# Retention: weighting the normed rows before the value projection, with the context's keys of all heads made first

## The chip, the cores and the metric

The kernel runs on one core of a Trainium2 chip. The metric is the device time of one execution in microseconds: the median of three runs of the kernel before is 1511.96 us (1507.57 to 1512.51). One further execution was taken with the hardware profiler; all durations below are from that one.

## The reference

Two transformer blocks of two layers each work on 256 tokens of 1024 features, in fp32. The first block (attention of four sorts, cross attention to a memory, a gated MLP with a short convolution) and most of the second (gated feed-forward layers, a convolution mixer) are not touched. The change lies in the first mixer of the second block, the retention. Cut to what matters:

```
ax = modulate(rms_norm(hx), ...)           # 256 x 1024, the tokens
ac = modulate(rms_norm(ctx), ...)          # 256 x 1024, the context
q, k, v, g = split(ax @ w_qkvg)            # 4 heads: q, k 256 wide, v, g 512 wide
kc, vc     = split(ac @ w_qkvg[:, D:4*D])  # keys and values of the context
q, k = rope(q), rope(k)
o = (q k^T * decay) v + (q kc^T * decay_ctx) vc       # per head, both directions
y = (silu(g) * o * rsqrt(mean(o*o) + eps)) @ w_o
hx = hx + g1 * y
```

Since v = ax @ Wv and vc = ac @ Wv with one matrix Wv, o is also ((q k^T * decay) ax + (q kc^T * decay_ctx) ac) @ Wv.

## The kernel before

Everything is kept feature-major: 1024 features are 8 tiles of 128 partitions, with the 256 tokens on the free axis. Each fp32 factor of a product is held as two tiles, a rounded high part (suffix h) and the rest (suffix l), and mm3 issues three TensorE products per tile: high with high, high with low, low with high.

Weights stream from HBM in pieces of 128x1024 in the order that `_plan` (L47) writes out by hand. SP loads a piece into one of five raw buffers (`Stream.dma`, L357). `Stream.split` (L369) makes the two parts: ScalarE copies to `wh`, VectorE subtracts to `wl`, into four slots; `Stream.get` (L386) hands a piece to the products and splits up to two or three pieces further ahead. A piece of 256 output columns holds four of the eight feature tiles, so a projection takes two pieces: `fm` (L487) does its 48 products into one PSUM bank, `fm_apart` (L492) into two banks, with some products 258 columns wide. `kouter` (L534) adds 48 products of an output matrix to the four accumulators. PSUM has four more banks for everything else (tag mm).

`after_piece` (L426) runs after each piece: it takes the next function from the list `hooks`, and every second piece it issues one product of the modulation parameters on VectorE (`ada_one`, L410, tile adaj) with its load.

The retention (from L1321) makes the normed rows `axs` of the tokens first, on ScalarE and VectorE with raised priority (`pre`, L1281, called at L1359). The context's rows `cxs` are there from the layer before. Then, for each of four heads: the load of the decay table `dec` (512 KB); keys and the first half of the values of both row sets with `both` (L1388), one piece serving `cxs` and `axs` in turn; the keys' rope; q and its rope; the second half of the values; the gates with Silu into `sg`; and as hooks, spread over the pieces that follow, the five steps of `ret_attention` (L1432): scores times decay (`ath`, `atl`), the weighted values in two halves, their norm's sums over single-column products, and the finish (the norm's factor spread by two small transposes, `sg` scaled and split into `soh`, `sol`). `ret_out(h - 1)` is called at the end of head h. In the first head `both` takes its four pieces at once (ahead) and does all of `cxs` ahead of all of `axs`.

The order within an engine is set by a planner when the program is built: it takes ready instructions by priority, which is the order in which the code issues them, apart from the raised ones.

Of the kernel before, what the change touches and what calls it, by code (L numbers as in the profile page):

```python
# [18 lines left out]
T = 256  # L19
# [27 lines left out]
def _plan():  # L47
# [29 lines left out]
    perm = _np.concatenate([half, half + 64])  # L77
    for h in range(4):
        add([("ret_w_qkvg_2", 0, 1024 + 256 * h + perm)], _ALL_K)
        for e in range(2):  # L80
            add([("ret_w_qkvg_2", 0, 2048 + 512 * h + 256 * e + _np.arange(256))], _ALL_K)
            if e == 0:
                add([("ret_w_qkvg_2", 0, 256 * h + perm)], _ALL_K)
        for e in range(2):
            add([("ret_w_qkvg_2", 0, 4096 + 512 * h + 256 * e + _np.arange(256))], _ALL_K)
        if h:
            for e in range(2):
                add([("ret_w_o_2", 0, _np.arange(D))], [4 * (h - 1) + 2 * e, 4 * (h - 1) + 2 * e + 1])
    for e in range(2):
        add([("ret_w_o_2", 0, _np.arange(D))], [12 + 2 * e, 13 + 2 * e])  # L90
# [184 lines left out]
def tile_two_blocks(ctx, tc, aps, out):  # L275
# [26 lines left out]
    def tt(out, a, b, op):  # L302
        V.tensor_tensor(out=out, in0=a, in1=b, op=op)  # L303
# [17 lines left out]

    X = cst_p.tile([128, KD, T], F32, name="X")
    CST = cst_p.tile([128, _NCST], F32, name="CST")
    VEC = cst_p.tile([128, _NVEC], F32, name="VEC")
    IDB = cst_p.tile([128, 128], BF16, name="IDB")
    MEMR = cst_p.tile([128, 2], F32, name="MEMR")
    CAUS = cst_p.tile([128, 128], BF16, name="CAUS")
# [4 lines left out]
    def cst(n):  # L332
        o, w = _CST[n]
        return CST[:, o:o + w]

# [4 lines left out]
    ones, ident, slt = cst("ones"), cst("ident"), cst("slt")  # L340
    ones_slt = CST[:, _CST["ones"][0]:_CST["ones"][0] + 256]

# [218 lines left out]
    WIDE, NARROW = 7 * (T + 64) + T + 64, 8 * T  # L561
# [107 lines left out]
    nc.sync.dma_start(out=CST, in_=aps["cst"])  # L669
# [125 lines left out]
    def layer(i, xs, nrm, last_gain, background=None, second=None):  # L795
        with ExitStack() as es:
# [210 lines left out]
            def fillers():  # L1007
# [4 lines left out]
                for t in range(2):  # L1012
                    act(VFX[:, t, :], o[t][:, 0:256], AF.Copy, scale=nrm.r[:, t:t + 1])
                    v = cp.tile([128, 128], F32, tag="vct", name="vct", bufs=2)
                    act(v, o[t][:, 256:384], AF.Copy, scale=nrm.r[:, t:t + 1])
                    vcs.append(v)
# [302 lines left out]
    cxs = box["cxs"]  # L1319

# [44 lines left out]
    def fm_part(o, e, h, l, n, xs):  # L1365

        hv = h.rearrange("p (k n c) -> p k n c", k=4, n=2)
        lv = l.rearrange("p (k n c) -> p k n c", k=4, n=2)
        for k4 in range(4):
            k = 4 * e + k4  # L1370
            for t in range(2):
                mm3(o[:, t * T:(t + 1) * T], hv[:, k4, t, :], lv[:, k4, t, :], xs[0](k), xs[1](k),
                    k == 0 and t == 0, k == 7)

    def tok_part(o, e, h, l, n, xs):

        hv = h.rearrange("p (k c) -> p k c", k=4)
        lv = l.rearrange("p (k c) -> p k c", k=4)
        for k4 in range(4):
            k = 4 * e + k4  # L1380
            for t in range(2):
                a, b = (x(k, t * 128, (t + 1) * 128) for x in xs)
                ov = o[:, t * 256:(t + 1) * 256]
                mm(ov, a, hv[:, k4, :], start=k == 0 and t == 0)
                mm(ov, a, lv[:, k4, :])
                mm(ov, b, hv[:, k4, :], stop=k == 7)

    def both(parts, ahead=False):  # L1388

        if ahead:  # L1390
            st.hold = st.n_get
            ws = [[st.get() for e in range(2)] for _ in parts]
            os_ = [[bank(), bank()] for _ in parts]
            for x, xs in enumerate((cxs, axs)):
                for f, w, o in zip(parts, ws, os_):
                    for e in range(2):
                        f(o[x], e, *w[e], xs)
                        if x:
                            after_piece()
            st.hold = None  # L1400
            return os_
        out = []
        for f in parts:
            o = [bank(), bank()]
            for e in range(2):
                w = st.get()
                for x, xs in enumerate((cxs, axs)):
                    f(o[x], e, *w, xs)
                after_piece()
            out.append(o)  # L1410
        return out

    def pair_tiles(tag, shape, bufs=1):
        at = 64 if tag in ("q", "at") else 128
        return [rp.tile(shape, F32R, tag=tag + e, name=tag + e, bufs=bufs, at=at) for e in "hl"]

    def rope2(tag, o):
        out = rp.tile([128, 2, T], F32, tag="ropo", name="ropo", bufs=1)
        a = rp.tile([128, 2, T], F32, tag="ropa", name="ropa", bufs=1)
# [12 lines left out]
    def ret_attention(h, q, kx, kc, vx, vc, sg, dec):  # L1432
        box_ = {}

        def scores():
            ath, atl = box_["at"] = pair_tiles("at", [128, 4, T], 1)
            for e, (kh, kl) in enumerate((kx, kc)):
                o = bank()
                for kt in range(2):
                    c = slice(kt * 128, kt * 128 + 128)  # L1440
                    for ab in range(2):
                        mm3(o[:, kt * T:(kt + 1) * T], kh[:, ab, c], kl[:, ab, c], q[0][:, ab, :], q[1][:, ab, :], kt == 0 and ab == 0, ab == 1)
                w = slice(2 * e, 2 * e + 2)
                at = rp.tile([128, 2, T], F32, tag="at", name="at")
                tt(at, o.rearrange("p (k t) -> p k t", k=2), dec[:, w, :], ALU.mult)
                split_psum(ath[:, w, :], atl[:, w, :], at)

        def values(e):
            ath, atl = box_["at"]
            o = bank()  # L1450
            for d2 in range(2):
                d = 2 * e + d2
                for kt in range(4):
                    vh, vl = (t[:, kt % 2, d * 128:(d + 1) * 128] for t in (vx, vc)[kt // 2])
                    mm3(o[:, d2 * T:(d2 + 1) * T], vh, vl, ath[:, kt, :], atl[:, kt, :], d2 == 0 and kt == 0, kt == 3)
            sq = rot_p.tile([128, 2, T], F32, tag="sq", name="sq")
            act(sq, o.rearrange("p (n t) -> p n t", n=2), AF.Square)
            box_["sq", e] = sq
            tt(sg[:, 2 * e:2 * e + 2, :], o.rearrange("p (n t) -> p n t", n=2), sg[:, 2 * e:2 * e + 2, :], ALU.mult)

        def sums():
            ss = rot_p.tile([128, 2, T], F32, tag="ss", name="ss")
            tt(ss, box_["sq", 0], box_["sq", 1], ALU.add)
            p = bank()
            for t in range(2):
                for e in range(2):
                    mm(p[:, t:t + 1], ss[:, e, t * 128:(t + 1) * 128], ones[:, 0:1], start=t == 0 and e == 0, stop=e == 1)
            box_["r"] = rsqrt(p[:, 0:2], 1.0 / 512.0)

        def finish():  # L1470
            R = spread(box_["r"])
            soh[h] = rp.tile([128, 4, T], F32R, tag="soh", name="soh", at=64)
            sol[h] = rp.tile([128, 4, T], F32R, tag="sol", name="sol", at=64)
            for e in range(2):
                q = slice(2 * e, 2 * e + 2)
                tt(sg[:, q], sg[:, q], R.unsqueeze(1).to_broadcast([128, 2, T]), ALU.mult)
                act(soh[h][:, q], sg[:, q], AF.Copy)
                tt(sol[h][:, q], sg[:, q], soh[h][:, q].bitcast(F32), ALU.subtract)

        return [scores, lambda: values(0), lambda: values(1), sums, finish]  # L1480

# [5 lines left out]

    for h in range(4):
        dec = rp.tile([128, 4, T], F32, tag="dec", name="dec", bufs=1)
        nc.sync.dma_start(out=dec, in_=aps["dec"][h].rearrange("p (k t) -> p k t", k=4))  # L1490
        kc, vx, vc = pair_tiles("kc", [128, 2, T]), pair_tiles("vx", [128, 2, 512]), pair_tiles("vc", [128, 2, 512])

        def keep_values(e, oc, ox):
            for v, o in ((vc, oc), (vx, ox)):
                split_psum(*(t[:, :, 256 * e:256 * e + 256] for t in v), o.rearrange("p (k c) -> p k c", k=2))


# [280 lines left out]
```

## Time and profile before

| | |
|---|---|
| median of three runs | 1511.96 us |
| the profiled execution | 1513.38 us, span 1511.6 us |
| TensorE products | busy 1478.4 us of the span, 12130 products |
| VectorE | busy 1185.9 us, 2297 instructions |
| ScalarE | busy 810.6 us, 1441 instructions |
| DMA | 292.95 MB, mean 194 GB/s |
| mean granted TensorE clock | 0.992 |

Times are microseconds from the start of the span. PE is TensorE, DVE is VectorE, ACT is ScalarE, SP is the engine that issues the loads. A product's duration is longer than the distance to the next one, because products overlap, so TensorE's busy time does not tell its rate; the distance of starts does.

### The profile page before, as it was taken

To read this page: it belongs to the slowest core of one execution; us is meant where nothing else is said; L and a number is where in the kernel's file an instruction comes from. 1 tells how busy PE (TensorE), PEld (TensorE's weight loads), DVE (VectorE), ACT (ScalarE), POOL (GpSimd) and SP (SyncE) were. 2 spreads that over 40 slices of the span, in tenths; PEclk is the share of its full clock that TensorE was granted. 3 is DMA by queue.
4 is the path that set the end of the run, shared out by engine and by line. 5 is a ranking of instruction groups with operands and counts; after the bars stand their busy time and mean duration, and the time that the engine had idled before them with its cause. 6 is when DMAs were issued, how large, how long until landed. Compare 5 with 4: busy or idle time off the path is not lost.

```text
span 1511.6 us, 30254 instructions
## 1 busy us (share of the span) xinstructions
PE 1478.4 (98%) x12130; PEld 1416.1 (94%) x12130; DVE 1185.9 (78%) x2297; ACT 810.6 (54%) x1441; POOL 0.2 (0%) x4
## 2 busy tenths in 40 slices
PE   8999999999999999999999999999999999999997
PEld 6877899999886889999999999999999999999997
DVE  7677789998888789999785766668977788885555
ACT  7455676565656467576543434335544465564443
POOL 0000000000000000000000000000000000000000
PEclk9999999999999999999999999999999999999998
DMA  8621446776562266587544656456788866556651
GB/s 299 223 78 31 150 169 207 251 239 205 190 223 85 89 204 227 180 273 266 184 165 168 194 169 209 153 183 208 261 297 290 296 186 191 182 181 196 195 190 64
DMA packets 81212, 292.95 MB, mean 194 GB/s; under 512 B 9136, under 2 KB 9136, under 8 KB 80944
## 3 DMA queue, kind: packets, MB, share of 16 engines
q1 hardware_dynamic: 81072, 291.03, 58.7%
q8 instruction: 95, 1.56, 0.4%
q14 instruction: 45, 0.37, 0.1%
HBM read 289.94 MB, written 1.05 MB: 193 GB/s over the span
## 4 chain that ended last, share of the span: by engine, by line
PE 88%; DVE 5%; DMA 3%; ACT 3%; issue 1%; SPq 0%; DVEq 0%; ACTq 0%
PE mm L297 58%; PE a L297 28%; DMA raw<-in_w_dram 2%; PE a L760 1%; DVE wl L303 1%; ACT wh L320 1%; DVE ss L303 1%; DVE xl L312 1%; DMA memx<-in_mem_dram 1%; DMA w<-in_cw_dram 1%; ACT xh L320 0%; DVE X L303 0%; DVE y L312 0%; ACT y L320 0%; ACT PT L761 0%
## 5 line engine op out<-in xcount | busy, mean ns | idle before, releaser
L303 DVE TENSOR_TENSOR wl<-raw,wh 128x1024 fp32r<-128x1024 f32 (+2 forms) x440 | 532.6, 1214 | 175.5 <-ACT wh L320 172.4
L320 ACT ACTIVATE wh<-raw 128x1024 fp32r<-128x1024 f32 (+2 forms) x440 | 459.9, 1050 | 346.1 <-PE mm L297 170.9
L297 PE MATMUL mm<-xh,wh 128*128 128x256 f32 (+1 forms) x2064 | 574.6, 279 | 2.7 <-ACT fj L320 2.6
L297 PE MATMUL mm<-xl,wh 128*128 128x256 f32 x2064 | 576.0, 279 | 0.0
L297 PE MATMUL mm<-xh,wl 128*128 128x256 f32 (+1 forms) x2064 | 573.6, 279 | 0.0
L297 PEld LDWEIGHTS mm<-xh,wh 128*128 128x128 f32 x2064 | 389.0, 189 | 3.9 <-ACT fj L320 3.0
L297 PEld LDWEIGHTS mm<-xl,wh 128*128 128x128 f32 x2064 | 389.2, 189 | 1.3 <-DVE xl L312 0.6
L297 PEld LDWEIGHTS mm<-xh,wl 128*128 128x128 f32 x2064 | 388.8, 189 | 0.0
L312 DVE SCALAR_TENSOR_TENSOR adaj<-adaw,CC 128x1024 bf16<-128x1024 f32 x112 | 136.4, 1218 | 0.1
L297 PE MATMUL mm<-wh,xh 128*128 128x256 f32 (+3 forms) x384 | 119.2, 311 | 7.0 <-ACT wh L320 7.0
L297 PE MATMUL mm<-wl,xh 128*128 128x256 f32 (+3 forms) x384 | 118.9, 310 | 0.0
L297 PE MATMUL mm<-wh,xl 128*128 128x256 f32 (+3 forms) x384 | 118.5, 309 | 0.0
L297 PE MATMUL a<-sh,wl 128*128 128x256 f32 x352 | 97.3, 276 | 1.3 <-DVE wl L303 1.3
L297 PE MATMUL a<-sh,wh 128*128 128x256 f32 x352 | 97.2, 276 | 0.0
L297 PE MATMUL a<-sl,wh 128*128 128x256 f32 x352 | 97.2, 276 | 0.0
L297 PE MATMUL a<-fsl,wh 128*128 128x256 f32 x352 | 96.9, 276 | 0.0
L297 PE MATMUL a<-fsh,wh 128*128 128x256 f32 x352 | 96.8, 276 | 0.0
L297 PE MATMUL a<-fsh,wl 128*128 128x256 f32 x352 | 96.6, 276 | 0.0
L297 PEld LDWEIGHTS mm<-wh,xh 128*128 128x128 f32 x384 | 72.8, 190 | 10.8 <-ACT wh L320 7.0
L312 DVE SCALAR_TENSOR_TENSOR y<-U,VEC,y 128x256 f32<-128x256 f32 x176 | 74.7, 479 | 4.6 <-ACT y L320 4.3
L297 PEld LDWEIGHTS mm<-wl,xh 128*128 128x128 f32 x384 | 72.7, 189 | 4.0 <-DVE wl L303 0.8
L297 PEld LDWEIGHTS mm<-wh,xl 128*128 128x128 f32 x384 | 72.7, 189 | 2.5
(308 smaller groups left out, 2422.0 us busy)
## 6 DMA issues: line engine op xcount, KB each, us to landing
raw<-in_w_dram SPq DMA_DIRECT2D x424, 512.0 KB, 4.1
adaw<-in_ada_dram SPq DMA_DIRECT2D x96, 512.0 KB, 4.5
raw<-in_w_dram SPq DMA_DIRECT2D x8, 416.0 KB, 4.0
raw<-in_w_dram SPq DMA_DIRECT2D x8, 384.0 KB, 4.4
memx<-in_mem_dram SPq DMA_DIRECT2D x4, 512.0 KB, 4.6
w<-in_cw_dram SPq DMA_DIRECT2D x4, 512.0 KB, 5.2
dec<-in_dec_dram SPq DMA_DIRECT2D x4, 512.0 KB, 4.5
X<-in_x_dram SPq DMA_DIRECT2D x4, 256.0 KB, 5.1
```

The costliest lines, as they stand in the source:

```text
L297: nc.tensor.matmul(out, lhsT, rhs, start=start, stop=stop, skip_group_check=True)
L303: V.tensor_tensor(out=out, in0=a, in1=b, op=op)
L312: return V.scalar_tensor_tensor(out=out, in0=a, scalar=s, in1=b, op0=op0, op1=op1, accum_out=accum_out)
L320: A.activation(out=out, in_=a, func=func, scale=scale, **kw)
L760: nc.tensor.transpose(pt[:, b:b + 128], Ps[u][:, h, kt * 128:(kt + 1) * 128], ident)
```

## The change

The values are no longer projected. Per head the scores weight the normed rows themselves: `weighted_rows` adds, over four tiles of tokens (two of `axs`, two of `cxs`), row tile times weight, for eight feature tiles, and splits the sums into the two parts `Y`. `values` then projects `Y` with the value weights by `fm`. For this the rows are needed with tokens on the partitions: `token_rows` transposes both parts of both row sets on TensorE, in groups of four 128x128, and ScalarE (high part) and VectorE (low part) copy them to `ctok` and `atok`.

The context's keys of all heads are made first, from their own copies of the key pieces; `kcs` keeps them. The key weights of each head are so streamed twice: the plan of this stage has 72 pieces instead of 64. The order within a head is then own keys, q, output of the head before (heads 1 and 2), scores, first gates, weighting, second gates, values; the outputs of heads 2 and 3 come last. The norm's sums and the finish remain hooks, now in the next head's keys and q. `fm_apart` remains for q of heads 0 and 2.

To make room, `dec` is half as large and loaded in two halves, the second into the same buffer after the first was used; the rope's buffers are those of the weighted scores (tag at); the gates lie in q's tiles; `soh` and `sol` lie in those of `Y`, for head 2 in those of the first context keys; `atok` lies in the rows' pool, in a slot whose tiles are 64 columns longer. The constants are split in two tiles and two loads, of which the second tile lives until the first block ends. In the first block, `vct` takes buffers of tag tok.

```diff
@@ _plan: order of the weights
+    for h in range(4):
+        keys(h)
     for h in range(4):
-        add([("ret_w_qkvg_2", 0, 1024 + 256 * h + perm)], _ALL_K)
-        for e in range(2):
-            add([("ret_w_qkvg_2", 0, 2048 + 512 * h + 256 * e + _np.arange(256))], _ALL_K)
-            if e == 0:
-                add([("ret_w_qkvg_2", 0, 256 * h + perm)], _ALL_K)
...
+        keys(h)
+        add([("ret_w_qkvg_2", 0, 256 * h + perm)], _ALL_K)
+        if h in (1, 2):
+            ret_out(h - 1)
+        gates(h, 0)
+        gates(h, 1)
+        vals(h, 0)
+        vals(h, 1)
+    ret_out(2)
+    ret_out(3)
...
+    def token_rows(xs, tok, t, kk):
+
+        for part, (x, o) in enumerate(zip(xs, tok)):
+            p = bank()
+            for j in range(4):
+                nc.tensor.transpose(p[:, j * 128:(j + 1) * 128], x(4 * kk + j, t * 128, (t + 1) * 128).bitcast(F32), ident)
+            w = o[:, t * D + kk * 512:t * D + kk * 512 + 512]
+            if part:
+                V.tensor_copy(out=w, in_=p)
+            else:
+                A.copy(out=w, in_=p)
...
+    def weighted_rows(ath, atl, Y):
+
+        for p in range(4):
+            o = bank()
+            for f2 in range(2):
+                f = slice((2 * p + f2) * 128, (2 * p + f2 + 1) * 128)
+                for kt in range(4):
+                    h, l = (t[:, (kt % 2) * D:(kt % 2 + 1) * D][:, f] for t in (atok, ctok)[kt // 2])
+                    mm3(o[:, f2 * T:(f2 + 1) * T], h, l, ath[:, kt, :], atl[:, kt, :], f2 == 0 and kt == 0, kt == 3)
+            split_psum(Y[0].pair(2 * p), Y[1].pair(2 * p), o.rearrange("p (n t) -> p n t", n=2))
...
+    for h in range(4):
+        if h % 2 == 0:
+            kc = half_tiles(f"kc{h}", [128, 4, T], 128)
+        o = fm(cxs)
...
+        split_psum(*kcs[h], o.rearrange("p (n t) -> p n t", n=2))
+        token_rows(cxs, ctok, h // 2, h % 2)
+
+    atok = [x.t[:, 16:16 + 2 * D] for x in xs_tiles()]
...
     for h in range(4):
...
+        kx = rope2("kx", fm(axs))
+        if h == 0:
+            for kk in range(2):
+                token_rows(axs, atok, 0, kk)
+        q = rope2("q", fm_apart(axs) if h % 2 == 0 else fm(axs))
         flush()
+        if h == 0:
+            for kk in range(2):
+                token_rows(axs, atok, 1, kk)
+        if h in (1, 2):
             if accs is None:
                 accs = four()
             ret_out(h - 1)
+        ath, atl = half_tiles("at_", [128, 4, T], 64)
+        scores(0, q, kx, decs[0], ath, atl)
+        nc.sync.dma_start(out=decs[1], in_=aps["dec"][h].rearrange("p (k t) -> p k t", k=4)[:, 2:4, :])
+        scores(1, q, kcs[h], decs[1], ath, atl)
+
+        sg = [t.bitcast(F32) for t in half_tiles("q", [128, 2, T], 64)]
+        act(sg[0], fm(axs).rearrange("p (n t) -> p n t", n=2), AF.Silu)
+        Y = tuple(Rows(t) for t in half_tiles("Y", [128, KD * T], 64))
+        weighted_rows(ath, atl, Y)
+        act(sg[1], fm(axs).rearrange("p (n t) -> p n t", n=2), AF.Silu)
+        sqs, box_ = [], {}
+        for e in range(2):
+            values(e, Y, sg, sqs)
+        hooks.append(lambda sqs=sqs, b=box_: sums(sqs, b))
+        hooks.append(lambda: None)
+        hooks.append(lambda h=h, sg=sg, b=box_: finish(h, sg, b))
+    ada_state["rate"] = 0
+    ret_out(2)
     flush()
```

## Rows read from the trace of the kernel before

**Rows 1.** The page: busy time by engine, and the chain that ended last, by engine.
```profile
PE 1478.4 (98%) x12130; PEld 1416.1 (94%) x12130; DVE 1185.9 (78%) x2297; ACT 810.6 (54%) x1441; POOL 0.2 (0%) x4
...
PE 88%; DVE 5%; DMA 3%; ACT 3%; issue 1%; SPq 0%; DVEq 0%; ACTq 0%
```

**Rows 2.** Stretches: length, busy us (instructions) of each engine, clock, DMA share, GB/s.
```profile
700.00:740.00 40.00, 40.00 (x356) 40.00 (x355) 36.06 (x60) 24.00 (x37) 0.00 (x0) 1.00 0.70 229
750.60:1036.80 286.20, 285.47 (x2462) 284.51 (x2462) 196.94 (x348) 110.15 (x153) 0.00 (x0) 1.00 0.55 178
755.00:772.60 17.60, 17.60 (x149) 17.37 (x149) 15.94 (x57) 7.59 (x15) 0.00 (x0) 1.00 0.28 88
```

**Rows 3.** Groups by line, 757 to 1042: count, busy us, mean ns, idle before.
```profile
L297 PE MATMUL mm<-wh,xh 128*128 128x256 f32 x256 | 71.2, 278 | 0.0
...
L297 PE MATMUL mm<-ath,vxh 128*128 128x256 f32 x32 | 8.9, 277 | 0.0
```

**Rows 4.** TensorE's timeline: start, us, engine, line, operation, tiles; ends of four stretches.
```profile
750.64 0.28 PE L297 MATMUL mm<-xh,wh 128*128 128x256 f32 x1
...
868.65 0.28 PE L297 MATMUL a<-soh,wh 128*128 128x256 f32 x1
...
871.37 0.28 PE L297 MATMUL mm<-ath,vxh 128*128 128x256 f32 x1
...
894.68 0.28 PE L297 MATMUL mm<-wh,xh 128*128 128x256 f32 x1
...
905.99 0.28 PE L297 MATMUL mm<-xh,wh 128*128 128x258 f32 x1
...
1036.82 0.28 PE L297 MATMUL mm<-xh,wh 128*128 128x258 f32 x1
```

**Rows 5.** TensorE's timeline: four transposes among wide products, in another stage.
```profile
405.26 0.60 PE L879 MATMUL mm<-CST,q 128*128 128x128 f32 x4
405.61 0.48 PE L297 MATMUL mm<-wh,xh 128*128 128x512 f32 x1
405.93 0.39 PE L297 MATMUL mm<-wl,xh 128*128 128x512 f32 x1
406.16 0.39 PE L297 MATMUL mm<-wh,xl 128*128 128x512 f32 x1
```

**Rows 6.** Line 879: the transposes' durations, ns min/median/max, first and last start.
```profile
L879 PE MATMUL mm<-CST,q x16: 272/273/312, 33.8 to 407.3; 128*128 128x128 f32 x16
```

**Rows 7.** TensorE's timeline: a norm's sums and the product behind them.
```profile
882.25 0.94 PE L297 MATMUL mm<-CST,ss 128*128 128x1 f32 x8
883.06 0.36 PE L297 MATMUL mm<-xh,wh 128*128 128x256 f32 x1
```

**Rows 8.** Groups by line of VectorE, 757 to 1042.
```profile
L312 DVE SCALAR_TENSOR_TENSOR adaj<-adaw,CC 128x1024 bf16<-128x1024 f32 x30 | 36.6, 1219 | 0.1
L303 DVE TENSOR_TENSOR ropo<-mm,RT 128x256 f32<-128x256 f32 x16 | 6.7, 418 | 2.8 <-PE mm L297 2.8
...
L303 DVE TENSOR_TENSOR ropo<-ropo,ropa 128x512 f32<-128x512 f32 x8 | 5.5, 687 | 0.1
```

**Rows 9.** VectorE's timeline at the start of the stage.
```profile
754.46 0.69 DVE L303 TENSOR_TENSOR ss<-ss,sq 128x512 f32<-128x512 f32 x1
...
770.59 2.06 DVE L312 SCALAR_TENSOR_TENSOR X<-X,VEC,R 128x256 f32<-128x256 f32 x5
...
777.58 3.49 DVE L303 TENSOR_TENSOR wl<-raw,wh 128x1024 fp32r<-128x1024 f32 x3
```

**Rows 10.** The tile dec: its loads, from issue to landing.
```profile
DMA to landing us min/median/max: 4.2/4.5/4.7
```

**Rows 11.** SP's timeline in the middle of the stage: issues of weight loads.
```profile
879.29 6.39 SPq L365 DMA_DIRECT2D raw<-in_w_dram  x2
```

**Rows 12.** Stretches behind the retention, columns as in rows 2.
```profile
1054.00:1058.00 4.00, 2.02 (x16) 1.82 (x15) 3.69 (x7) 2.87 (x9) 0.00 (x0) 0.97 1.01 377
1058.00:1062.00 4.00, 4.00 (x24) 4.00 (x23) 3.65 (x9) 0.06 (x1) 0.00 (x0) 0.61 0.96 321
```

More of the change, by code (lines that the diff above doesn't have):

```diff
@@ L1363, in tile_two_blocks @@
         stt(X[:, k, :], X[:, k, :], gf[:, k:k + 1], nrm.R, ALU.mult, ALU.mult)
[L1365 to L1411, printed above, removed]
@@ L1428, in rope2 @@
         return hl
-    soh, sol = {}, {}
[L1432 to L1480, printed above, removed]
@@ new lines, in token_rows, with scores @@
+    def token_rows(xs, tok, t, kk):
[8 more added lines that the diff above has]
+                A.copy(out=w, in_=p)
+    def scores(e, q, keys, dec, ath, atl):
+        kh, kl = keys
+        o = bank()
+        for kt in range(2):
+            c = slice(kt * 128, kt * 128 + 128)
+            for ab in range(2):
+                mm3(o[:, kt * T:(kt + 1) * T], kh[:, ab, c], kl[:, ab, c], q[0][:, ab, :], q[1][:, ab, :], kt == 0 and ab == 0, ab == 1)
+        w = slice(2 * e, 2 * e + 2)
+        at = rp.tile([128, 2, T], F32, tag="at", name="at")
+        tt(at, o.rearrange("p (k t) -> p k t", k=2), dec, ALU.mult)
+        split_psum(ath[:, w, :], atl[:, w, :], at)
@@ L1486, in ret_out, with values @@
             kouter(lambda f: (soh[h][:, 2 * e + f, :], sol[h][:, 2 * e + f, :]), accs, h == 0 and e == 0, h == 3 and e == 1)
-    for h in range(4):
[L1489 to L1495, printed above, removed]
-        a, b = both([fm_part, tok_part], h == 0)
-        split_psum(*kc, a[0].rearrange("p (n t) -> p n t", n=2))
-        kx = rope2("kx", a[1])
-        keep_values(0, *b)
-        q = rope2("q", fm_apart(axs))
-        keep_values(1, *both([tok_part])[0])
-        sg = rp.tile([128, 4, T], F32, tag="sg", name="sg", bufs=1)
+    def values(e, Y, sg, sqs):
+        o = fm(Y)
+        sq = rot_p.tile([128, 2, T], F32, tag="sq", name="sq")
+        act(sq, o.rearrange("p (n t) -> p n t", n=2), AF.Square)
+        sqs.append(sq)
+        tt(sg[e], o.rearrange("p (n t) -> p n t", n=2), sg[e], ALU.mult)
@@ new lines, in sums, with finish @@
+    def sums(sqs, box_):
+        ss = rot_p.tile([128, 2, T], F32, tag="ss", name="ss")
+        tt(ss, sqs[0], sqs[1], ALU.add)
+        p = bank()
+        for t in range(2):
+            for e in range(2):
+                mm(p[:, t:t + 1], ss[:, e, t * 128:(t + 1) * 128], ones[:, 0:1], start=t == 0 and e == 0, stop=e == 1)
+        box_["r"] = rsqrt(p[:, 0:2], 1.0 / 512.0)
+    def finish(h, sg, box_):
+        R = spread(box_["r"])
+        if h == 2:
+            soh[h], sol[h] = half_tiles("kc0", [128, 4, T], 128)
+        else:
+            soh[h], sol[h] = (t[:, 0:4 * T].rearrange("p (k t) -> p k t", k=4) for t in half_tiles("Y", [128, KD * T], 64))
+        for e in range(2):
+            q = slice(2 * e, 2 * e + 2)
+            tt(sg[e], sg[e], R.unsqueeze(1).to_broadcast([128, 2, T]), ALU.mult)
+            act(soh[h][:, q], sg[e], AF.Copy)
+            tt(sol[h][:, q], sg[e], soh[h][:, q].bitcast(F32), ALU.subtract)
@@ L1505, in tile_two_blocks @@
+    for h in range(4):
+        decs = []
         for e in range(2):
+            dec = rp.tile([128, 2, T], F32, tag="dec", name="dec", bufs=1)
+            decs.append(dec)
             if e == 0:
-                for f, o in enumerate(fm_apart(axs)):
-                    act(sg[:, f, :], o, AF.Silu)
-            else:
-                act(sg[:, 2 * e:2 * e + 2, :], fm(axs).rearrange("p (n t) -> p n t", n=2), AF.Silu)
-        flush()
-        steps = ret_attention(h, q, kx, kc, vx, vc, sg, dec)
```

59 lines of the change are left out of this document (31 added, 28 removed).

## The prediction

> **What bounds the kernel now.** I read the page first. TensorE is busy for 98% of the span and the chain that ended last runs through it for 88% [rows 1], so time can only be won by giving TensorE less to do or by filling its gaps. Then the table by stretches: the retention stage, 750.6 to 1036.8 us, has TensorE busy for 285.5 of 286.2 us at the full granted clock, with VectorE at 196.9 us (69%) and ScalarE at 110 us [rows 2]. So this stage has no gaps to fill: it is a count of products. The two rows that carry most of what is edited are in the groups by line [rows 3]: 256 products of each of three kinds form the values of both row sets (768 in all), and 32 of each of six kinds weight them (192). Last I read the timeline for the price of a product. The mean of 278 ns in those groups is a latency, since products overlap; what counts is the distance of starts. 24 products of 256 columns start between 868.65 and 871.37, so 113.3 ns each; 96 start between 894.68 and 905.99, so 117.8 ns each [rows 4]. The stream has these two paces. In this stage it falls into the slower one behind single-column sums or small transposes, and comes back while a run of 258-column products (fm_apart) passes.
>
> The stage in full: 2400 products at 113.3 ns are 271.9 us of the 286.2 between 750.64 and 1036.82 [rows 4]. Of the other 14.3 us some 7 are the norms' single-column sums and their spreads (one set of eight takes from 882.25 to 883.06 [rows 7]; there are six such sets and as many spreads), the rest, about 7, is the slower pace.
>
> **The change part by part.**
>
> *Products.* Per head, before: 96 for keys, 192 for values, 48 for q, 96 for gates, 24 for scores, 48 for weighting, 96 for the output, 600 in all. After: 48 for the context's keys, 48 for own keys, 48, 96 and 24 as before, 96 to weight the rows (8 feature tiles x 4 token tiles x 3), 96 for the values of the sums, 96 for the output, 552. Four heads lose 192 products; at 113.3 ns that is -21.8 us, all on the path, since TensorE has no slack.
>
> *Transposes.* Weighting sums over tokens, so the rows must stand with tokens on the partitions: 64 transposes of 128x128, in 16 groups of four. In the trace four transposes hold the stream from 405.26 to 405.61, and the product behind them keeps the next one 0.32 us away instead of 0.23 [rows 5]: 0.44 us per group, +7.0 us. Bounds: 5.6 (nothing behind them) to 17.5 us (64 x 273 ns [rows 6], nothing overlapped). I take the row, which is the same operation among the same kind of products. The Trainium skill ("TensorE: Matmul & The Clock Gate", Part 4: PE-mode transpose) speaks against this part: it measures about 275 ns for one in a kernel, and says that transposes do not keep the clock up. By that, end to end, they would cost 17.6 us and the gain would all but vanish; the row of four in 0.35 us disagrees, so I give this under 2 in 100, inside the case "eaten".
>
> *Pace.* Before, fm_apart runs twice in every head; after, only for q of heads 0 and 2, and in head 0 transposes follow it. The slower pace costs 4.5 ns per product: at most 9.9 us if all 2208 go so, 0 if none. I take two thirds of the most and the runs of 258 with it, 9 us against 7 now: +2.0 us, between -7 and +3.
>
> *The start of the stage.* This is where I expect a gap. Before, the first four weight pieces serve 48 products each, so TensorE lives on them while VectorE makes the normed rows. After, a piece of context keys serves 24 products, 2.7 us. VectorE worked 15.94 us in 755.0 to 772.6 [rows 2], without a single split of weights between 754 and 775. Of that, 15.3 us stay (one 0.6 us key split is counted below). Until piece 8 is split it must add four splits at 1.14 us (three take 3.49 [rows 9]), 4.6 us, and for heads 0 and 1 a key split and a copy of transposed rows each, 4 x 0.6 = 2.4 us. From 755.1 [rows 9] that ends at 777.4 without a pause. TensorE wants piece 8 after 168 products (19.0 us), six groups of transposes (2.6 us) and the norm's sums (1.9 us, two sets and their fringes): at 774.2. So it waits 3.2 us: +3.2. ScalarE, busy 7.59 us of the 17.6, has room for its four splits. Bounds: 0, if the eight scalings of X (five take 2.06 us [rows 9]) are put behind the splits; 9 us, if two further ada products (1.22 us each [rows 8]) and the pauses of the norm's chain go ahead of them too, and if the clock falls. The one long wait behind this stage shows that last part: TensorE is busy for 2.02 us of 1054 to 1058, and then the granted clock is 0.61 over 1058 to 1062 [rows 12], part of it at the lower level, 1.2 GHz, and only 24 products pass instead of some 34: another 1.2 us. The Trainium skill ("TensorE: Matmul & The Clock Gate", HAM oscillation) warns of idle gaps that throttle the array again; the trace agrees with 0.61.
>
> *Starts of the heads.* Keys and q are now 96 products in a row (10.9 us) where they stood among 192 of values. In that time VectorE must do four splits (4.6 us), two ada products (2.4), the keys' rope (four of 0.42 and two of 0.69, 3.1 [rows 8]), the sums' chain (about 2, an estimate from one of 0.69 and a dozen on two columns) and the finish (four of 0.69, 2.8): 14.9 us, 4 too many. Two pieces split ahead, 2.7 us of products each, just cover that. The gates' values now lie in q's tiles, so the split of q waits for the finish of the head before, and the scores behind it on TensorE wait too: for heads 1 and 2 the output products (10.9 us) stand between, for head 3 only gates that can be taken early. I take 0.5, 0.5 and 1: +2.0 us, between 0 and 8.
>
> *Half decay tables.* The second half is asked for when the scores of the first are weighted, into the same buffer. It waits for that VectorE instruction on SP, and all weight loads issued later stand behind it; they have up to five raw buffers in hand. Landing takes 4.2 to 4.7 us [rows 10]; with 0.7 us ahead, and 1.9 us behind it for the second weighting and its split, 7.1 us. Beside it lie the other 12 products of scores (1.4 us) and the first gates (5.4 us), 6.8 us, then the second gates if they are taken early (5.4 us). I cost it at nothing; if that cover goes, see the slower rival.
>
> *The rest.* Eight more pieces: 8 splits on ScalarE and VectorE, 4 MB of loads where the DMA share is 0.55 [rows 2]; 16 row copies; four more ada products in this stage, and four fewer later. VectorE goes from 197 to about 216 us of 279, 77%; in 700 to 740 it is 90% busy and TensorE loses nothing [rows 2], so the mean is harmless and only bunching counts, which is priced above. The split of the constants' load, their pool and the shared buffer of vct touch stages with a wait of microseconds elsewhere; 0, between -1 and +1.
>
> Sum: -21.8 + 7.0 + 2.0 + 3.2 + 2.0 = -7.6 us. The profiled execution took 1513.4 us (span 1511.6), so it becomes 1505.8; the median of the three runs shown is 1.4 us lower than it, so I predict **1504.5 us**.
>
> **The rivals.**
> *A: TensorE stays full.* For it: 286 us without a gap, and rows 2 at 90% VectorE. Then the last three terms go and the pace stays: -14.8 us, 1497. Against it: VectorE's sum at the start.
> *B: eaten.* The start costs 8 us, the heads 4: -21.8 + 7.0 + 2.0 + 12 = -0.8 us, 1511. For it: between 1054 and 1058 VectorE is 92% busy and TensorE loses half of the time [rows 12]. Against it: VectorE recovers in the 10.9 us of each weighting, which needs no pieces.
> *C: slower, by the half tables.* One place, four times: the load of the second half. SP issues in order, and two weight loads take 6.39 us to get out in the middle of a head [rows 11]. If the half table stands 3.2 us behind one and the second gates are not taken ahead, each head waits 7.1 + 3.2 - 6.8 = 3.5 us: +14, so +6.4 in all, 1518; behind two, 6.7 us a head, 1531. It decides from 1.9 us a head on (nothing left to win), and is slower than can be told from 3 us. For it: the buffer is single. Against it: the order was interleaved before, output products and weighting in runs of 24 at 113.3 ns, so ready products are moved ahead.
>
> **How the numbers follow.** A measurement of this kernel can tell about 0.3%, 4.5 us, from no change. Forecast (4.5 to 12 us won) 0.41, A 0.17, B 0.23, C 0.19. Faster is the forecast and A, 0.58; same is B, 0.23; slower is C, 0.19. The likeliest case alone spans 1500 to 1507.5. The range goes from A with a little pace won, 1494, to C, 1519.
>
> **What would show it.** Right: 2208 products and 64 transposes in the stage, some 279 us long; TensorE's waits name the weight splits of VectorE, once for about 3 us before the own keys; VectorE is full for 25 us there. Wrong: no wait at the start (A); waits on the weighted scores in every head, ended by the table's load (C); transposes with starts over 0.2 us apart.

## The result, and the profile after

The changed kernel takes 1521.62 us (median of 20 runs) where the kernel before, timed on the same chip, takes 1510.77: a ratio of 1.0073 [1.0057, 1.0089]. It is slower, by some 11 us, where I forecast 7.6 us less. The profiled execution after is the shortest of its 20 runs (1510.65 us, span 1508.8), so its span must not be compared with that of before; the stretches within it can. A second profile of the same kernel (after_again below) has a span of 1520.5.

The page after, the lines of [rows 1]:

```profile
PE 1463.8 (97%) x12002; PEld 1397.6 (93%) x12002; DVE 1196.7 (79%) x2313; ACT 821.6 (54%) x1453; POOL 0.2 (0%) x4
...
PE 85%; DVE 7%; ACT 3%; DMA 3%; issue 2%; SPq 0%; DVEq 0%; ACTq 0%
```

The 128 fewer instructions on TensorE are the 192 products less and 64 transposes more of the prediction. But TensorE's share of the chain fell by three points and VectorE's rose by two: more of the path now runs through waits.

The retention stage after, in the columns of [rows 2], whole and at its two worst places (the context's rows, and the start of head 3):

```profile
747.40:1037.10 289.70, 275.73 (x2334) 271.13 (x2333) 212.24 (x374) 121.54 (x165) 0.00 (x0) 0.98 0.60 198
...
768.00:772.00 4.00, 2.21 (x18) 1.74 (x16) 4.00 (x12) 2.62 (x5) 0.00 (x0) 1.00 0.26 103
772.00:774.00 2.00, 1.20 (x6) 0.72 (x6) 2.00 (x3) 0.01 (x1) 0.00 (x0) 0.93 0.00 0
774.00:778.00 4.00, 3.62 (x20) 3.62 (x21) 4.00 (x7) 0.58 (x1) 0.00 (x0) 0.61 0.58 193
...
968.00:972.00 4.00, 1.20 (x11) 1.00 (x9) 4.00 (x9) 2.18 (x3) 0.00 (x0) 0.96 0.34 122
972.00:976.00 4.00, 0.49 (x2) 0.49 (x3) 4.00 (x8) 0.63 (x1) 0.00 (x0) 0.50 0.56 157
976.00:980.00 4.00, 4.00 (x27) 4.00 (x27) 2.31 (x4) 0.23 (x1) 0.00 (x0) 0.68 0.88 293
```

The stage was to shrink from 286.2 to some 279 us; it is 289.7. TensorE is idle for 14 us of it (0.7 before), VectorE is 73% busy on the mean, but full (4.00 of 4.00, 2.00 of 2.00) at both places. After each the granted clock falls to 0.61 and 0.50: a part of the products runs at the lower level, 1.2 GHz.

TensorE's waits in 740 to 1040 us after (tile and line that waited, who ended it; us in all, times, longest; two more, 0.7 us together, are left out):

```profile
PE mm L305 <- ACT qh L328: 7.1, 2, 6.3
PE mm L1403 <- ACT cth L1408: 1.6, 1, 1.6
PE mm L305 <- DVE at_l L311: 1.1, 2, 0.7
PE mm L1403 <- ACT xh L1408: 0.9, 2, 0.7
PE mm L305 <- DVE kc0l L311: 0.8, 1, 0.8
PE a L305 <- DVE Yl L311: 0.7, 2, 0.4
PE a L305 <- ACT Yh L328: 0.5, 1, 0.5
PE mm L305 <- DVE wl L311: 0.4, 1, 0.4
```

Nearly half of it is one wait, before the scores of head 3 (qh). The weighted scores (at_l), rival C's place, are 1.1 us. No wait of the list is ended by a load, so the eight pieces more cost TensorE nothing that shows here.

The distance of starts sorts the stage's time. For each product I take 113.3 ns as its price; what lies over it is pace (up to 126 ns), a slow start (190 to 235 ns), or a wait (the rest). The transposes stand from their start to the next instruction's, waits included.

| us | before | after | difference | forecast |
|---|---|---|---|---|
| products at 113.3 ns (2400, 2208) | 271.9 | 250.2 | -21.7 | -21.8 |
| pace | 4.4 | 3.0 | -1.4 | +2.0 |
| slow starts | 1.5 | 5.3 | +3.8 | in the start |
| waits of products | 2.6 | 12.6 | +10.0 | +5.2, start and heads |
| transposes with their waits | 0 | 12.6 | +12.6 | +7.0 |
| single-column sums, spreads | 5.7 | 6.0 | +0.3 | 0 |
| stage | 286.2 | 289.7 | +3.5 | -7.6 |

The count of products came out as forecast; their row uses the forecast's own price, so it tests the count alone. The slow starts are only in part the clock: before has its 1.5 us of them at a granted clock of 1.00 [rows 2], behind single-column products (behind the one at 883.06 in [rows 7] the next starts at 883.26) or ahead of a wait. After, some 2.5 of the 5.3 us are products 0.21 us apart at the two places above, at the lower clock. What was lost is waiting in the main, and the clock behind it. The transposes' own price is in TensorE's timeline of head 0: groups start 0.44 us apart, as forecast from [rows 5], so 7.0 of the 12.6 us are theirs.

```profile
786.89 0.60 PE L1403 MATMUL mm<-KEEP,xh 128*128 128x128 f32 x4
787.33 0.60 PE L1403 MATMUL mm<-KEEP,xl 128*128 128x128 f32 x4
787.77 0.60 PE L1403 MATMUL mm<-KEEP,xh 128*128 128x128 f32 x4
```

What VectorE does while TensorE waits for q in head 3, from its timeline (the wait is 968.92 to 975.51):

```profile
968.64 0.68 DVE L311 TENSOR_TENSOR kxl<-ropo,kxh 128x512 fp32r<-128x512 f32 x1
969.24 0.68 DVE L311 TENSOR_TENSOR kc0l<-qh,kc0h 128x512 fp32r<-128x512 f32 x1
...
970.45 1.21 DVE L320 SCALAR_TENSOR_TENSOR adaj<-adaw,CC 128x1024 bf16<-128x1024 f32 x1
...
971.59 0.42 DVE L311 TENSOR_TENSOR ropo<-mm,RT 128x256 f32<-128x256 f32 x1
...
972.92 1.21 DVE L311 TENSOR_TENSOR wl<-raw,wh 128x1024 fp32r<-128x1024 f32 x1
974.05 0.68 DVE L311 TENSOR_TENSOR ropo<-ropo,ropa 128x512 f32<-128x512 f32 x1
```

The own keys' split, the finish of head 2 (kc0l), an adaptation slice (adaj), q's rope with a weight split in its middle: all queue on VectorE, and only the last row lets q's copy begin. TensorE meanwhile stands at the scores, with 192 products behind them in its order that need no q: 96 of gates, and 96 of the output of head 2, whose values are complete from 970.5 on.

And at the start of the stage, while TensorE waits for a bank to be copied out and for the keys' split:

```profile
769.16 2.84 DVE L320 SCALAR_TENSOR_TENSOR X<-X,VEC,R 128x256 f32<-128x256 f32 x7
771.93 0.67 DVE L311 TENSOR_TENSOR kc0l<-mm,kc0h 128x512 fp32r<-128x512 f32 x1
772.53 0.67 DVE L1406 CAST ctl<-mm 128x512 fp32r<-128x512 f32 x1
```

Seven scalings of X, which nothing wants before the end of the stage, go ahead of the split and the copy. The longest wait there, 1.6 us, is ended by a copy of ScalarE (cth); x_late below shows that it hangs on the scalings too.

### The profile page after: what moved, and what is told of

Read it like the earlier page. It is cut to its first block, busy times and chain, and to the rows that moved or that the text cites. A ratio compares the mean times of both kernels' runs of the same rounds, so it can differ in the third digit from the quotient of the medians.

```text
span 1508.8 us, 30064 instructions
## 1 busy us (share of the span) xinstructions
PE 1463.8 (97%) x12002; PEld 1397.6 (93%) x12002; DVE 1196.7 (79%) x2313; ACT 821.6 (54%) x1453; POOL 0.2 (0%) x4
## 4 chain that ended last, share of the span: by engine, by line
PE 85%; DVE 7%; ACT 3%; DMA 3%; issue 2%; SPq 0%; DVEq 0%; ACTq 0%
PE mm L305 55%; PE a L305 28%; DVE wl L311 2%; ACT wh L328 1%; PE a L773 1%; DVE xl L320 1%; DVE ss L311 1%; DMA raw<-in_w_dram 1%; DMA memx<-in_mem_dram 1%; DMA w<-in_cw_dram 1%; ACT xh L328 1%; DMA dec<-in_dec_dram 0%; DVE adaj L320 0%; DVE X L311 0%; ACT PT L774 0%
## 5 line engine op out<-in xcount | busy, mean ns | idle before, releaser
L311 DVE TENSOR_TENSOR wl<-raw,wh 128x1024 fp32r<-128x1024 f32 (+2 forms) x448 | 540.9, 1212 | 168.2 <-ACT wh L328 167.3
L328 ACT ACTIVATE wh<-raw 128x1024 fp32r<-128x1024 f32 (+2 forms) x448 | 468.3, 1050 | 358.4 <-PE mm L305 203.8
L305 PE MATMUL a<-xh,wh 128*128 128x256 f32 (+1 forms) x240 | 70.4, 293 | 0.6 <-ACT vct L328 0.6
L305 PE MATMUL a<-xl,wh 128*128 128x256 f32 x240 | 68.6, 286 | 0.0
L305 PE MATMUL a<-xh,wl 128*128 128x256 f32 (+1 forms) x240 | 68.2, 285 | 0.0
L305 PEld LDWEIGHTS a<-fsh,wh 128*128 128x128 f32 x352 | 65.9, 188 | 0.2 <-ACT fsh L328 0.2
L305 PEld LDWEIGHTS a<-fsl,wh 128*128 128x128 f32 x352 | 66.1, 188 | 0.0
L305 PEld LDWEIGHTS a<-sh,wh 128*128 128x128 f32 x352 | 66.1, 188 | 0.0
```

The costliest lines, as they stand in the source:

```text
L305: nc.tensor.matmul(out, lhsT, rhs, start=start, stop=stop, skip_group_check=True)
L328: A.activation(out=out, in_=a, func=func, scale=scale, **kw)
```

## The experiments

Each kernel was timed beside the kernel before on the same chip, in 6 to 12 executions; the figure given is the ratio of the two, with its 95% interval. "Stage" is the stretch from the first context key to the feed-forward network in the profile (before 286.2).

**after_again**, the changed kernel once more.

> The changed kernel unaltered, for a second profile beside that of the record. Theory (waits): TensorE waits twice in the retention stage, some 5 us behind the context keys and some 6.6 us between q and the scores of head 3, each with a stretch at the lower clock behind it; both stand again in this profile, within 1 us, and the stage takes 289 to 293 us. Rival (elsewhere): the stage is as long as before or shorter and the loss lies in the first block, where the constants and vct were moved; then the stretch up to the first context key is more than 4 us longer than before's 750.6 us.

Measured: 1.0068 [1.0043, 1.0093], stage 292.7. The loss stands; the stage differs by 3 us between two profiles of one kernel, so I lean on differences over that, and on the timings.

**x_late**: the eight scalings of X from the start of the stage to behind head 0's weighting.

```
+        if h == 0:
+            for k in range(KD): stt(X[:, k, :], ...)   # was ahead of the context keys
```

> The eight scalings of X on VectorE (3.2 us) are issued behind head 0's weighting instead of ahead of the context keys. Theory (VectorE is full at the start of the stage): the wait behind the fourth piece of context keys shrinks by about 3 us, and with it what the lower clock takes: 3 to 5 us won, 1517 to 1519 us. Rival (TensorE waits there for PSUM banks or a load, not for VectorE): no change.

Measured: 1.0040 [1.0026, 1.0053]. From the stage's start to the norm's sums of head 0 it takes 88.3 us where the unaltered kernel took 92.1 and 91.2. TensorE's waits at that place, 1.6, 0.8 and 0.4 us after (cth, kc0l and wl in the list above), shrink to one, and the granted clock stays at 1.00 there:

```profile
PE mm L1401 <- ACT cth L1406: 0.6, 1, 0.6
```

So the scalings on VectorE made most of these waits. The whole stage is 289.0 all the same: heads 1 and 2 take 61.0 and 62.2 us in this profile (60.4 and 60.3 after), most of it slower pace.

**gates_first**: in head 3 the first gate's products are issued ahead of the scores (`g0 = fm(axs)` in front, its Silu where it was).

> In head 3 alone the first gate projection (48 products, 5.4 us) is issued ahead of the scores. Theory (waits): the wait of 6.6 us before the scores of head 3 shrinks to 1.2 us or less and the stretch at the lower clock behind it goes, so 5 to 8 us are won against the changed kernel: 1514 to 1516 us. Rival (the chain of q is what counts, the products merely move): the wait comes back before the weighting, and the time stays within 2 us of the changed kernel's 1521.6.

Measured: 1.0051 [1.0032, 1.0069], stage 291.7: no shorter than after, and the timings cannot tell it from after either. The wait of 6.3 us falls apart without vanishing. TensorE's waits, 960 to 990 us:

```profile
PE mm L305 <- ACT qh L328: 1.6, 1, 1.6
PE mm L305 <- ACT at_h L328: 1.2, 1, 1.2
PE mm L305 <- DVE ql L311: 0.7, 1, 0.7
```

The gate that had covered the weighted scores (at_h) had been used up in front. Here one cover (ready products that TensorE does while an operand is still being made) did not serve two waits.

**out_split**: half of the output products of head 2 (48) ahead of head 3's scores, half where all were, at the stage's end.

```
+        if h == 3: ret_out(2, [0])
         scores(...)
...
-    ret_out(2)
+    ret_out(2, [1])
```

> The changed kernel with half of the output products of head 2 (48, one pair of feature tiles, with their pieces of weights) issued ahead of the scores of head 3; the other half stays behind the last head. Theory (the wait in front of head 3's scores is there because no ready product stands in TensorE's order, and the half clock follows from it): 5.4 us of products fill the 6.5 us wait, the clock stays up, 5 to 8 us less: 1509 to 1513. Rival (VectorE sets the pace of head 3, as gates_first showed, and the wait moves to the weighted scores or to the finish at the stage's end): 1515 to 1518.

Measured: 1.0059 [1.0037, 1.0081], stage 290.9. The wait before the scores is gone, and the time is back at the end, where these products had covered the finish of head 3. Waits at 1015 to 1042 us, then stretches:

```profile
PE a L307 <- ACT Yh L330: 2.5, 1, 2.5
PE a L307 <- DVE Yl L313: 0.9, 1, 0.9
PE mm L649 <- DVE ry L322: 0.7, 1, 0.7
```

```profile
1020.00:1028.00 8.00, 3.90 (x24) 3.28 (x24) 6.46 (x18) 2.67 (x4) 0.00 (x0) 0.87 0.50 181
1028.00:1032.00 4.00, 4.00 (x20) 4.00 (x20) 0.00 (x0) 0.96 (x1) 0.00 (x0) 0.50 0.12 45
```

**dec_once**, against rival C: no load of the second half of the decay table; both scores use the first.

> The changed kernel without the loads of the second half of the decay table: both scores of a head are weighted with the first half (the second half is left out of the computation). This takes rival C away whole, and the waits of TensorE on the second half of the weighted scores with it. If these waits (0.9, 0.6 us in heads 1 and 2, and what the loads do to the queue of SP) are all there is to it: 1 to 3 us under the changed kernel, 1514 to 1516 on the scale of 1508 for before. If the half tables are what made the change slow: 6 us or more under it, 1511 or less.

Measured: 1.0074 [1.0048, 1.0099], stage 289.3. The waits on the weighted scores (at_l, 0.7 and 0.4 us) vanish from heads 1 and 2 and nothing is won. Rival C is out.

**tr_twice**: every transpose twice into the same bank.

> The changed kernel with every transpose of the retention done twice into the same bank (64 more, nothing else). My term for 64 transposes was 7.0 us, worked out from four in 0.35 us and a slower product behind them. If four more in a group cost only their own 0.35 us: +5.6 us; if the transposes stand in the shadow of VectorE's waits (half of the groups stand where TensorE waits anyhow): +2 to +4 us; if one costs its 275 ns: +17 us. So 1520 to 1525 by the first two, 1535 by the last.

Measured: 1.0069 [1.0046, 1.0091], stage 293.6. TensorE's timeline, where all four groups of eight run without a wait, and the stretch around them:

```profile
798.05 1.04 PE L1403 MATMUL mm<-KEEP,xh 128*128 128x128 f32 x8
798.92 1.04 PE L1403 MATMUL mm<-KEEP,xl 128*128 128x128 f32 x8
799.79 1.04 PE L1403 MATMUL mm<-KEEP,xh 128*128 128x128 f32 x8
800.67 1.04 PE L1403 MATMUL mm<-KEEP,xl 128*128 128x128 f32 x8
```

```profile
798.00:802.00 4.00, 3.70 (x34) 3.47 (x33) 3.79 (x8) 2.67 (x4) 0.00 (x0) 1.00 0.46 139
```

Eight per 0.87 us, 0.109 us each, at a granted clock of 1.00. 64 more are 7 us of TensorE, yet the stage grew by 0.9 to 3.9 us (on 292.7 and 289.7): the rest lies in time in which TensorE waited anyhow. The Trainium skill ("TensorE: Matmul & The Clock Gate", Part 4: PE-mode transpose) has about 275 ns for one in a kernel, and says that the full clock does not engage for them. The trace agrees with the 275 ns as a duration (273 ns in [rows 6], 272 here) and not as a price, which is the 0.109 us between starts. This row of 32 was entered at a clock of 1.00 and kept it for its 3.5 us; what a longer one would do no run shows.

**pools_only, vct_only, consts_t1**: the kernel before with edits outside the retention alone. pools_only has all (constants in two tiles and loads, the pool, vct in the tok buffers); vct_only the last; consts_t1 the others, with vct in part of a t1 buffer, as its own two no longer fit.

```
-  v = cp.tile([128, 128], F32, tag="vct", name="vct", bufs=2)
+  v = cp.tile([128, 512], F32, tag="tok", name="vct", bufs=3)[:, :128]    # the change
+  v = sp.tile([128, 384], F32, tag="t1", name="vct")[:, :128]             # consts_t1, vct_t1
```

> The kernel before with only the edits outside the retention: constants in two tiles and two loads, their pool closed behind the first block, vct in the buffers of tag tok. Theory (waits in the retention): same time as before, within 2 us. Rival (placement and loads of the constants): 4 to 10 us slower than before.

> The kernel before with one line changed: the token rows of the context values in the full-attention layer (vct) lie in the rotating tok buffers (three of 512 columns) and no longer in two buffers of their own. Theory 1, the loss of pools_only comes from shared buffers: these copies now rotate with the other token tiles, so tiles of layer 1 wait for each other; +3 to +5 us over before (ratio 1.002 to 1.0035), the layer-1 attention some 2 us longer than its 220.2 us. Theory 2, it comes from the constants being loaded and held in two tiles: this kernel is within 1 us of before. Theory 3, the 4 us are an accident of alignment that no part has alone: both this run and consts_t1 lie at +1 to +3 us.

> The kernel before with the constants in two tiles and two loads and the pool that is closed after layer 1, and vct in a part of the t1 buffer of another pool (its own two buffers no longer fit). Theory 1 (shared tok buffers): within 1.5 us of before. Theory 2 (the constants): +3 to +5 us (ratio 1.002 to 1.0035), and the loss is then at the start of layer 0, where the second load lands later.

Measured: 1.0028 [1.0008, 1.0047], 1.0020 [1.0006, 1.0033], 0.9998 [0.9982, 1.0013]. The constants, with vct in t1, cost nothing that can be told; vct in tok costs some 3 us (1 to 5 by the interval).

**vct_t1**: the changed kernel with that one line.

> The changed kernel with one line other: vct in a part of the t1 buffer and not in the rotating tok buffers. Theory (the tok buffers cost what vct_only showed, 2 to 4 us, in the first two layers): 1512.5 to 1515 on the scale of 1508 for the kernel before, where the changed kernel itself is at 1517 to 1519. Rival (the first layers have slack there that only the timing of single runs fills): 1516 to 1519, no difference.

Measured: 1.0030 [1.0012, 1.0048], stage 289.7 as without this edit. The profile has the gain in the attention of layer 1, which only this line and the place of the constants touch. That stretch after, and in vct_t1:

```profile
378.20:600.20 222.00, 216.25 (x1561) 187.94 (x1560) 191.54 (x491) 135.78 (x291) 0.00 (x0) 0.99 0.52 169
```

```profile
377.30:595.50 218.20, 213.87 (x1561) 185.87 (x1560) 190.88 (x491) 136.05 (x291) 0.00 (x0) 1.00 0.51 173
```

The same instructions, 3.8 us apart. Not all of that is the buffer: after has a dip of the clock in this stretch and vct_t1 has none. The same place after, and in vct_t1:

```profile
435.80:439.20 3.40, 3.40 (x18) 3.40 (x18) 2.43 (x9) 1.59 (x4) 0.00 (x0) 0.50 0.48 194
```

```profile
434.90:438.30 3.40, 3.17 (x28) 2.73 (x27) 2.71 (x13) 1.72 (x5) 0.00 (x0) 1.00 0.80 313
```

Such a dip comes with either buffer, and before has it too. Over all profiles: eleven with vct in tok take 220.2 to 223.1 us there (median 222.0), seven with it in t1 216.6 to 220.4 (218.2), before 220.2. Among the profiles with a dip (four and two) the medians lie 2.7 us apart, among those without (seven and five) 3.4 us. By the timings the edit wins more, some 6 us (1.0030 against 1.0073 and 1.0068); where the rest of that lies is not shown.

**ada_later**: the adaptation slices (1.22 us on VectorE each) put off during the context keys and in head 3.

> The changed kernel with the slices of the adaptation (VectorE work of 1.23 us each) put off during the context keys and in head 3, and taken in heads 0 to 2 alone. Theory VectorE is the late engine in front of the splits of q in head 3 and at the stage's start: one slice less in each place brings the wait before the scores of head 3 from 6.5 to about 5 us and the first part of the stage from 92 to about 90 us; 1514 to 1515.5 on the scale of 1517 for the changed kernel. Rival, the wait in head 3 is made by the chain of ScalarE and VectorE operations itself (rope, copy, subtract) with nothing to be put off: no difference, 1516.5 to 1518.

Measured: 1.0062 [1.0042, 1.0082], stage 287.7. The first part gains (87.4 us against 92.1 and 91.2), so the slices were late there as the scalings were. Head 3's wait stays (6.1 us), as the rival said, and the slices come back between the halves of the feed-forward network. That stretch after, and in ada_later:

```profile
1222.80:1338.80 116.00, 115.83 (x975) 115.03 (x974) 96.85 (x180) 69.27 (x155) 0.00 (x0) 1.00 0.57 183
```

```profile
1228.00:1346.70 118.70, 117.25 (x975) 115.86 (x974) 102.92 (x194) 70.53 (x157) 0.00 (x0) 1.00 0.62 196
```

**gates_both**: order alone. Both gates of every head between its scores and the weighting, in head 3 the first of them ahead of the scores.

```
+        g0 = fm(axs) if h == 3 else None
         scores(...)
         act(sg[0], g0 or fm(axs), Silu)
+        act(sg[1], fm(axs), Silu)
         weighted_rows(ath, atl, Y)
-        act(sg[1], fm(axs), Silu)
```

> The changed kernel with order alone edited: both gates of every head before the weighting, and in head 3 the first of them before the scores. The scalings of X, the adaptation slices and vct stay as in the changed kernel. If order of ready products is what head 3 and the weighted scores lacked: the stage 5 to 8 us shorter (282 to 285 us), ratio to before 1.002 to 1.0035. If the slices on VectorE in head 3 are needed as well (the wait then goes on, as with gates_first): 1.005, stage 289 to 291 us.

Measured: 1.0026 [1.0010, 1.0041], stage 282.6; head 3 takes 51.2 us from the norm's sums of head 2 to its own (55.9 after). With VectorE's work unchanged (212.24 us after), order gives 7 us of the stage back, 10 against after_again. The stage, then the start of head 3:

```profile
746.00:1028.70 282.70, 273.79 (x2335) 269.53 (x2334) 211.96 (x375) 121.56 (x165) 0.00 (x0) 0.99 0.60 203
...
968.00:972.00 4.00, 2.80 (x24) 2.60 (x23) 4.00 (x7) 2.24 (x3) 0.00 (x0) 1.00 0.54 159
972.00:976.00 4.00, 3.60 (x31) 3.60 (x32) 4.00 (x6) 0.35 (x1) 0.00 (x0) 1.00 0.84 287
976.00:980.00 4.00, 4.00 (x38) 4.00 (x37) 3.39 (x7) 2.19 (x3) 0.00 (x0) 1.00 0.89 297
```

VectorE is as full as after, TensorE has products, and the clock stays at 1.00. The wait for q is 1.6 us where it was 6.3.

**The combinations.** combo_t1 is x_late, gates_first, ada_later and vct_t1 in one; combo2 has out_split in place of gates_first; combo3 is combo_t1 with the order of gates_both; combo4 is combo3 with a slice at every piece during the values; combo4_again is combo4 once more, on another chip.

> The changed kernel with four edits: the eight scalings of X behind head 0's weighting, the adaptation slices out of the context keys and of head 3, head 3's first gate ahead of its scores, vct in t1. If the losses add up (x_late -3.4, gates_first -1, slices -2, vct -2 to -4): 1507 to 1510 on the scale of 1517 for the changed kernel, that is level with before (1507.7) or 1 to 2 us over it. Rival, the stage is held by VectorE as a whole and what is put off is late somewhere else: 1512 to 1514, as x_late alone.

> combo_t1 with the split output products of out_split in place of the gate ahead of head 3's scores. If the wait of head 3 is filled without a new one: 3 to 6 us under combo_t1, 1502 to 1505 on the scale of 1508.5 for the kernel before, faster than both kernels. If combo_t1 had filled it already and VectorE holds head 3: 1506.5 to 1508, as combo_t1.

> combo_t1 with both gates of every head issued between its scores and the weighting (10.9 us of products that need nothing new), where the second stood behind the weighting. The waits on the weighted scores (0.4 us in heads 1 and 2, 2.7 us in head 3, with the half clock behind it) should go: stage 279 to 281 us against 283.1, 3 to 4 us less, 1503 to 1505 on the scale of 1508 for before (ratio 0.9965 to 0.998). Rival (VectorE is late as such, and the wait moves to the values or to the finish at the end): as combo_t1, ratio 0.999.

> combo3 with the adaptation slices that combo_t1 puts off taken during the values of each head (one a piece in place of one every second piece). ada_later showed the price of putting them off: 118.8 us against 116.0 between the two halves of the feed-forward network. If that is right, 2 to 3 us less than combo3; if VectorE has no room during the values, the finish of the heads comes later and it is as long as combo3 or 1 to 3 us longer.

> combo4 unaltered, on another chip, because its first measurement had few runs: ratio 0.993 to 0.997. A ratio near combo3's 0.9974 would mean that the slices taken during the values bring nothing.

| | ratio to before | stage |
|---|---|---|
| combo_t1 | 0.9990 [0.9975, 1.0005] | 283.1 |
| combo2 | 1.0026 [1.0007, 1.0045] | 284.7 |
| combo3 | 0.9974 [0.9956, 0.9992] | 275.4 |
| combo4 | 0.9949 [0.9929, 0.9969] | 278.1 |
| combo4_again | 0.9952 [0.9932, 0.9972] | 278.9 |

The stage in combo3, columns as above:

```profile
746.10:1021.50 275.40, 270.94 (x2334) 267.49 (x2333) 200.26 (x353) 121.15 (x165) 0.00 (x0) 1.00 0.56 189
```

In combo2 the waits at the stage's end are those of out_split. combo3 has the same 2334 instructions on TensorE as after, 14.3 us shorter, at a clock of 1.00. combo3 and combo4 beat both kernels, combo4 by 7 to 8 us under before. That is about what I had forecast for the change, but by chance: it took edits that the change does not have. Its stage is longer than combo3's, but the stretch of ada_later's rows is 116.0 us (116.6 the second time) and not 118.1; combo4's interval overlaps combo3's, so that this edit adds anything is not shown.

## Why the prediction was wrong

*Products, pace.* 192 products fewer, as counted; the pace came out at -1.4 us for +2.0, inside its bounds. The idea that fewer products are time won holds: combo3's stage is 10.8 us under before's, and combo4's, with all of VectorE's work in it, 7 to 8 us.

*Transposes.* The term of 7.0 us was right (0.44 us a group). What I did not see is that a group also needs a PSUM bank that ScalarE or VectorE must empty. Of the 5.6 us over that term after, 2.5 are such waits (cth and xh in the list); most of the rest are waits of the products behind a group, for the keys' split, a weight split and q. In combo3 1.7 us are left (8.7 us in all).

*The start of the stage: mis-sized.* I took 3.2 us. The first part takes 92.1 us after and 84.8 in combo3, so it lost at least 7.3 us: inside my upper bound of 9, which had further adaptation slices and the clock in it. About 3.9 of the 7.3 are the transposes' waits of the paragraph above. Both causes on VectorE show alone: 88.3 us without the scalings in front (x_late), 87.4 without the slices (ada_later). The place was not the forecast one: I had TensorE wait once, for the weight splits of the own keys; it waited among the context keys, for copies and a key split, and only 0.4 us for a weight split. I had priced a sum over the whole stretch, as if VectorE would work in the order of need. It works in the order planned.

*The starts of the heads: the step that failed.* "... for head 3 only gates that can be taken early. I take 0.5, 0.5 and 1." I had head 3 lose 1 us. It lost 5.6 (55.9 against combo3's 50.3). Heads 1 and 2 lost 1.0 and 0.7 us (60.4 and 60.3 against 59.4 and 59.6), which is no more than they differ between two profiles of one kernel (61.5 and 61.6 in after_again). The gates could have been taken early and were not: the scores stood ahead of them in TensorE's order, and it stood at them for 6.3 us. I had read from before that ready products are moved ahead; its runs of 24 products without a gap [rows 4] were no proof of it for this place. gates_both shows that order is enough to win most of it back (51.2 us), gates_first that one gate is not, out_split that taking the cover from the end is not.

*The rest: failed.* "... the shared buffer of vct ... 0, between -1 and +1." It costs 3.0 us over its own buffers (vct_only), and in the attention of layer 1 some 3 us over t1 by the profiles with a like clock. I had argued that this stage waits for microseconds elsewhere; that TensorE waits there anyhow (some 4 us before) did not make the edit free. By which instructions the shared buffer costs its time is not shown.

*The rivals.* C was the rival that said slower, and the kernel is slower, but not by C's way: its waits are 1.1 us in all, and nothing is won without the second loads (dec_once). That the direction fits is luck. B, start 8 and heads 4, is closest in kind with 7.3 and 7.3, but it had the kernel come out level: vct is not in it, nor all of what head 3 lost.

*The sum as measured.* combo3's stage, -10.8; the start +7.3, the heads +7.3, together with the stage's end (-0.4) the 14.2 of 14.3 us between combo3 and after; vct +3.0. That is +6.4 us, and +9.4 with the stage of the second profile, where the timings say +8.6 to +13.4 (0.0057 and 0.0089 of 1510.77). With the first profile's stage 2 us or more of the loss are not found, with the second's the sum lies inside the interval; vct at the 6 us of vct_t1's timing would close the gap as well. What makes two profiles of one kernel differ by 3 us in the stage stays open too; the second is longer by 1.0 to 1.2 us in each of heads 1 to 3.

## What to carry to other kernels

When work is cut from an engine that was never idle, look for the instructions that now stand closer to their producers: here the gain was kept only where ready work stood ahead of them in the engine's own order (gates_both), and each wait needed a cover of its own. A cover moved from one wait to another moved the loss (out_split, gates_first). And an edit that only shares a buffer is to be timed by itself: here it cost some 3 us, where the whole change was to win 7.6.

## What the runs showed of the chip

The lower clock came behind a cluster of short waits as well as behind one long one: 769 to 774.4 us after has idle times of 1.6, 0.8 and 0.4 us around twelve transposes, and products behind it start 0.21 us apart, at a granted clock of 0.61 over 774 to 778. With one wait of 0.6 us there (x_late) it stayed at 1.00. A busy TensorE is no sign of a full clock: in out_split it is busy for 4.00 of 4.00 us, behind waits of 2.5 and 0.9 us, at a granted clock of 0.50. 32 transposes in a row ran at 1.00 (tr_twice), 0.109 us apart, where one lasts 272 ns.
